# A triangular inverse, the RG-LRU's products and the rotations on VectorE alone, with a list schedule made in rounds

## The chip, the cores and the metric

The kernel runs on one core of one Trainium2 chip. The metric is the device time of one execution in microseconds. Each run of a kernel gives one time; a profiled execution also gives a trace and a page. Engine names in the rows: PE is TensorE (PEld its weight loads), DVE VectorE, ACT ScalarE, POOL GpSimd, SP SyncE.

## The reference

Two layers of a token mixer are computed for 128 context tokens and 512 latent tokens together (640 tokens, five tiles of 128). A layer does, in float32:

```python
mod = silu(c) @ w_mod + b_mod                 # shift, scale, gate
h = rms_norm(x) * (1 + scale) + shift
p = h @ w_in                                  # 640 x 3456
ya = rwkv7(p)         # two directions, a state of 64x64 for each of 4 heads
yb = window_attention(rope(p))                # and a sink
yc = rg_lru(conv(p))                          # two directions
yd = differential_attention(rope(p))
y = concat(ya, yb, yc, yd, each times its SiLU gate) @ w_out
x = x + gate * rms_norm(y)
```

The RWKV-7 recurrence s <- s*diag(w) - (s kk)(kk a)^T + v k^T is not run token by token: in chunks of 64 tokens it becomes matmuls and the inverse of a unit triangular 64x64 matrix for each chunk, head and direction.

## The kernel before

**Work.** Weights come as chunks of 512 KB through two `raw` buffers (`raw`, `weight`, L528 to L538), are split into a high and a low float32r half (`split`, L519: ScalarE or GpSimd rounds, L522 or L524, and VectorE subtracts, L525) and multiplied three times (hi*hi, hi*lo, lo*hi; `gemm_tm`, `gemm_fm`, all recorded by `mm`, L352). These dense matmuls are most of TensorE's work. `tm_chunk` makes six chunks of 256 columns token by token; chunks 2 and 4 (keys and queries of the differential attention) are copied from PSUM by ScalarE (L662) and rotated by `rope` (L579, five instructions at L586, L590, L591) on GpSimd for the four latent tiles; chunks 0 and 1 are rotated on VectorE straight from PSUM.

**Modulation.** `mod_chunk` and `mod_columns` (L412 to L432) multiply the two conditioning vectors with `w_mod`: eight matmuls a chunk with 32 columns of the array (`raw,cs` or `ZA,cs`), a copy, then two narrow products (`const,s`), from which VectorE writes `gadd` and `gmul` (L441, L443, L444). In layer 0 those for layer 1 are made between the dense matmuls.

**The inverse** (`rwkv_inv`, L1251). For each direction the attention matrices (FA,F matmuls of `rwkv_mats`, L1194, masked on VectorE at L1210) leave SBUF for DRAM (L1262) and come back with one 32x32 diagonal block a partition (L1264, 80 blocks). There a substitution runs over 31 columns: a product (L1278) and a subtraction (L1280) of outer products. `CUT = 24` splits each step's columns: a part goes to GpSimd, the rest (up to eight) to VectorE. The result is transposed (L1281), stored (L1282, L1283), reloaded (L1286, L1288) and joined to 64x64 by 32x32 matmuls (L1303, L1312). `rwkv_keys`, `rwkv_solve`, `rwkv_chain` and `rwkv_read` follow.

**RG-LRU** (`lru`, L1002). `LRU_CONV`, `LRU_Q`, `LRU_U`, `LRU_S` and `LRU_H` say for each half or direction whether GpSimd (1) or VectorE (0) does the convolution's taps, sqrt's argument, the gated input, its product and the sum of directions. On GpSimd a three-operand step is two instructions (`stt`, L990).

**Order.** `body` builds the program twice. The first build is only read: `plan` (L1873) collects each instruction's engine, a length by formula (`_length`), and its dependencies, and `_list_schedule` (L1800) lays them on the five in-order queues. An instruction's rank is the length of the longest chain from it to the end; at each moment the engine that is free takes the ready instruction of the highest rank. On TensorE it prefers to stay with matmuls that use 64 rows or fewer, or with those that use more (`half`; a change costs `TURN` = 0.1). It knows the shared time of VectorE and GpSimd (`port`). `follow` then ties each engine's instructions of the second build to that order. SP's queue issues all DMAs.

Of the kernel before, what the change touches and what calls it, by code (L numbers as in the profile page):

```python
# [101 lines left out]
DP1 = 1000  # L102
E_BANKS = (3, 6), (2,), (7,), (0, 1)
D_BANKS = (2, 3, 6, 7), (4,)
CUT = 24
F_WO = (9, 12)
LRU_BANKS = (4, 5)
D_ORDER = (4, 0, 1, 2, 3)
# [1 line left out]
F_TILES = (6, 7, 0, 1)  # L110
F_AT = (0, 2, 5, 8)
F_RO = (1, 3, 4, 5, 6)
LRU_CONV = (0, 1)
LRU_Q = (1, 1, 1, 1)
LRU_U = (0, 1, 0, 1)
LRU_S = (0, 1, 0, 1)
LRU_H = (1, 1)
W_F = 0
OUT_BANKS = (0, 2)
W_O = (0, 1, 0, 1)  # L120
# [139 lines left out]
class Net:  # L260
# [362 lines left out]
    def tm_evac(self, l, ch, i, ps):  # L623
        A, nc, O = self.A, self.nc, self.O
        tk = slice(i * 128, i * 128 + 128)
        if ch == 0:
            A.activation(self.bv[:, i, :], ps[:, 128:256], AF.Copy)
            r = self.t1([128, 128])
            if i == 4:
                A.activation(r, ps[:, 0:128], AF.Copy)  # L630
                nc.sync.dma_start(O["nwk"][l], r)
                nc.sync.dma_start(O["nwv"][l], self.bv[:, 4, :])
            else:
                self.rope(self.V, r, ps[:, 0:128], i, 2, 64, C_C64, C_S64)

            def rest():
                pt = self.pt([128, 128])
                self.P.transpose(pt, r, self.ident)
                A.activation(self.kT[:, i * 128:i * 128 + 128], pt, AF.Copy)
            return rest  # L640
        elif ch == 1:
            r = self.t1([128, 256])
            if i == 4:
                A.activation(r, ps, AF.Copy)
            else:
                self.rope(self.V, r, ps, i, 4, 64, C_C64, C_S64)

            def rest():
                pt = self.pt([128, 2, 128])
                for g in range(2):  # L650
                    self.P.transpose(pt[:, g, :], r[:, 128 * g:128 * g + 128], self.ident)
                A.activation(self.qT[:, :, tk], pt, AF.Copy)
            return rest
        elif ch in (2, 4):
            dst = self.at(self.turn("st", M_ST), [128, 256])
            if i == 4:
                A.activation(dst, ps, AF.Copy)
                if ch == 2:
                    nc.sync.dma_start(O["ndk"][l], dst)
            else:  # L660
                x = self.t1([128, 256])
                A.activation(x, ps, AF.Copy)  # L662
                self.rope(self.G, dst, x, i, 8, 32, C_C32, C_S32)
            nc.sync.dma_start(self.qkv[1 if ch == 2 else 0, :, i, :], dst)
        elif ch == 3:
            dst = self.at(self.turn("st", M_ST), [128, 256])
            A.activation(dst, ps, AF.Copy)
            nc.sync.dma_start(self.qkv[2, :, i, :], dst)
            if i == 4:
                nc.sync.dma_start(O["ndv"][l], dst)  # L670
        else:
            for p in range(2):
                rw = slice(64 * p, 64 * p + 64)
                A.activation(self.SV[rw, i, p], ps[rw, :].rearrange("p (h e) -> p h e", h=4), AF.Copy)
# [1049 lines left out]
SAME = 0.04  # L1724
# [36 lines left out]
    return 0.145 + 0.00104 * n  # L1761


def _shares(i):

    if _engine(i) == "Pool":
# [2 lines left out]
            and type(i).__name__[4:] not in ("Memset", "Reciprocal", "TensorReduce"))  # L1769


TURN = 0.1
STAY = 2.0


# [21 lines left out]
            self.k, self.busy = self.k + 1, 0.0  # L1797


def _list_schedule(names, engine, length, deps, size, half, port):  # L1800

    succ, left = {n: [] for n in names}, {}
    for n in names:
        left[n] = len(deps[n])
        for x in deps[n]:
            succ[x].append(n)
    seen = lambda n, s: (0.0 if engine[n] == "PE" else SAME) if engine[n] == engine[s] != "SP" else SEEN.get(engine[n], 0.0)
    todo, tail, free = [n for n in names if not left[n]], {}, dict(left)
    for n in todo:
        for s in succ[n]:  # L1810
            free[s] -= 1
            if not free[s]:
                todo.append(s)
    for n in reversed(todo):
        own = length[n] + (2.0 + size[n] / 320 if engine[n] == "SP" else 0.0)
        tail[n] = own + max((tail[s] + seen(n, s) for s in succ[n]), default=0.0)
    rank = {n: (-tail[n], k) for k, n in enumerate(names)}
    queues, turned, held = ENGINES + (None,), False, {"DVE": 0.0, "Pool": 0.0}
    clock = _Clock()
    idle, link, ready = dict.fromkeys(queues, 0.0), 0.0, dict.fromkeys(names, 0.0)  # L1820
    come, here, out = {e: [] for e in queues}, {e: [] for e in queues}, []
    for n in names:
# [2 lines left out]
    while len(out) < len(names):  # L1825
# [6 lines left out]
        if e == "PE":  # L1832
            if half[n] != turned:
# [5 lines left out]
                    heapq.heappush(here[e], (rank[n], n))  # L1839
                    n = x[1]  # L1840
                else:
                    t += TURN
            turned = half[n]
        if n in port:
            until = held["Pool" if e == "DVE" else "DVE"]
# [16 lines left out]
        if e == "SP":  # L1862
            link = max(link, t + 1.2) + size[n] / 320
            end = link + 0.6
        for s in succ[n]:
            ready[s] = max(ready[s], end + seen(n, s))
            left[s] -= 1
            if not left[s]:
                heapq.heappush(come[engine[s]], (ready[s], rank[s], s))
    return out  # L1870


def plan(I, O):  # L1873
# [13 lines left out]
    trace = {i.name: i for i in trace}  # L1887
    engine = {n: _engine(trace[n]) for n in names}
    length = {n: 0.08 if engine[n] == "SP" else _length(trace[n]) for n in names}
    half = {n: engine[n] == "PE" and list(trace[n].ins[0].ap)[0][1] <= 64 for n in names}  # L1890
    port = {n for n in names if _shares(trace[n])}
    size = {n: math.prod(k for _, k in trace[n].outs[0].ap) / 256 if engine[n] == "SP" else 0.0 for n in names}
    deps = {n: {d for d, _ in nc.dependency_edges(n)} & known for n in names}
# [52 lines left out]
```

## Time and profile before

| | |
|---|---|
| runs shown | 1174.52, 1188.54, 1189.49 us; median 1188.54 |
| the profiled execution | 1178.09 us, span 1176.3 us |
| granted TensorE clock, mean | 0.934 |
| busy: PE, PEld, DVE, ACT, POOL | 1056.7, 899.5, 701.6, 515.0, 381.7 us |
| chain that ended last, by engine | PE 62%, DVE 11%, ACT 8%, issue 8%, DMA 7%, POOL 3% |
| HBM read, written | 82.90 MB, 15.47 MB |

The span runs from the first to the last instruction. TensorE's ends are modelled and overlap, so a busy TensorE may still have slack; the granted clock tells which part of the time it ran at 2.4 and which at 1.2 GHz. A wait is put down to the releaser that came last.

### The profile page before, as it was taken

The page shows a single profiled execution, that of the slowest core. Times are in us where ns is not written, and L with a number is a line of the kernel's source. Part 1 is how long each engine was busy: PE and PEld are TensorE (multiplying, and loading weights), DVE is VectorE, ACT ScalarE, POOL GpSimd, SP SyncE. Part 2 cuts the span into 40 slices and gives each one's busy share as a digit, 9 for nine tenths or more (in the row PEclk, how much of TensorE's full clock was granted, in tenths as well). Part 3 has the DMA queues.
Part 4 walks back from the last instruction along what each step waited for, and adds up shares of the span by engine and source line. Part 5 has one row for each costly group of instructions (what it writes and reads, how often), then busy time and mean ns, then how long its engine had stood idle before and what let it go on. Part 6 is the DMA issues. An engine that isn't in the chain of part 4 may idle for free.

```text
span 1176.3 us, 24765 instructions
## 1 busy us (share of the span) xinstructions
PE 1056.7 (90%) x10166; PEld 899.5 (76%) x10166; DVE 701.6 (60%) x1646; ACT 515.0 (44%) x1154; POOL 381.7 (32%) x465
## 2 busy tenths in 40 slices
PE   4999988869988998899997999889997998999996
PEld 2798766758876786677996987688886787777796
DVE  4823477526567569478566248672667656967622
ACT  5426433124243547556226473223424354766410
POOL 0032443505780010015123366450577002112312
PEclk9999989769987999889998999987999899999898
DMA  9421344540323031014312102433031303101311
GB/s 367 163 70 69 120 128 118 178 118 9 86 76 81 7 104 43 19 36 139 109 72 90 55 30 83 113 108 95 13 92 65 81 7 120 45 19 37 126 55 54
DMA packets 60225, 99.97 MB, mean 85 GB/s; under 512 B 30736, under 2 KB 38672, under 8 KB 60112
## 3 DMA queue, kind: packets, MB, share of 16 engines
q1 hardware_dynamic: 60112, 98.39, 26.1%
q8 instruction: 80, 1.31, 0.5%
q14 instruction: 33, 0.27, 0.1%
HBM read 82.90 MB, written 15.47 MB: 84 GB/s over the span
## 4 chain that ended last, share of the span: by engine, by line
PE 62%; DVE 11%; ACT 8%; issue 8%; DMA 7%; POOL 3%; SPq 1%; POOLq 0%; ACTq 0%; DVEq 0%
PE banks L352 55%; PE banks L892 2%; PE banks L848 2%; DMA raw<-in_w_tm 1%; PE banks L783 1%; DMA F<-inv 1%; DMA inv<-F 1%; ACT FA L881 1%; DVE F L1280 1%; DMA raw<-in_w_m 1%; PE banks L1235 1%; POOL F L1562 1%; SPq L1286 1%; DMA inv<-ZA 1%; DVE WP L525 1%
## 5 line engine op out<-in xcount | busy, mean ns | idle before, releaser
L352 PE MATMUL banks<-HA,WP 128*128 128x384 f32 (+1 forms) x768 | 208.5, 339 | 7.7 <-DVE mt L701 5.4
L352 PE MATMUL banks<-WP,HA 128*128 128x256 f32 x880 | 186.8, 300 | 14.2 <-ACT WP L522 10.6
L352 PEld LDWEIGHTS banks<-WP,HA 128*128 128x128 f32 x880 | 145.1, 200 | 27.7 <-ACT WP L522 11.1
L352 PEld LDWEIGHTS banks<-HA,WP 128*128 128x128 f32 x768 | 140.0, 202 | 17.8 <-DVE mt L701 6.3
L352 PE MATMUL banks<-HB,WP 128*128 128x384 f32 (+1 forms) x384 | 126.5, 335 | 1.5 <-DVE rq L367 1.1
L352 PE MATMUL banks<-WP,HB 128*128 128x256 f32 x440 | 119.2, 298 | 0.0
L525 DVE TENSOR_TENSOR WP<-raw,WP 128x1024 fp32r<-128x1024 f32 x44 | 56.4, 1282 | 62.6 <-ACT WP L522 60.5
L352 PEld LDWEIGHTS banks<-WP,HB 128*128 128x128 f32 x440 | 82.8, 200 | 4.1 <-issue 3.3
L352 PEld LDWEIGHTS banks<-HB,WP 128*128 128x128 f32 x384 | 76.5, 201 | 5.2 <-issue 2.1
L352 PE MATMUL banks<-WQ,HA 128*128 128x256 f32 x320 | 77.3, 302 | 2.0 <-DVE WQ L525 0.9
L522 ACT ACTIVATE WP<-raw 128x1024 fp32r<-128x1024 f32 x46 | 48.4, 1059 | 64.4 <-PE banks L352 42.0
L352 PE MATMUL banks<-FA,F 64*128 64x128 f32 (+3 forms) x768 | 66.7, 277 | 5.0 <-DVE FA L1177 2.2
L352 PE MATMUL banks<-F,ZA 64*64 64x64 f32 (+2 forms) x1440 | 62.4, 228 | 5.9 <-DMA F<-inv 5.1
L352 PEld LDWEIGHTS banks<-F,ZA 64*64 64x64 f32 (+2 forms) x1440 | 55.1, 140 | 14.8 <-issue 6.8
L703 POOL TENSOR_TENSOR F<-F,mt 128x256 f32<-128x256 f32 (+1 forms) x16 | 19.2, 1199 | 137.3 <-DVE mt L701 119.8
L352 PEld LDWEIGHTS banks<-WQ,HA 128*128 128x128 f32 x320 | 58.0, 202 | 6.1 <-issue 3.1
L878 DVE TENSOR_REDUCE dm<-banks 128x2 f32<-128x1280 f32 (+1 forms) x40 | 50.9, 1273 | 19.0 <-PE banks L352 18.8
L352 PEld LDWEIGHTS banks<-FA,F 64*128 64x128 f32 (+2 forms) x768 | 47.9, 158 | 17.1 <-issue 7.5
L881 ACT ACTIVATE FA<-banks,dm 128x640 f32<-128x640 f32 (+1 forms) x80 | 56.4, 709 | 8.1 <-DVE dm L878 6.1
L352 PE MATMUL banks<-F 128*64 128x128 f32 (+3 forms) x256 | 44.0, 358 | 5.2 <-ACT F L763 3.8
L352 PE MATMUL banks<-WQ,HB 128*128 128x256 f32 x160 | 47.4, 301 | 0.0
L352 PE MATMUL banks<-HA,WQ 128*128 128x384 f32 (+1 forms) x192 | 45.6, 310 | 0.5 <-ACT K L733 0.5
(340 smaller groups left out, 2637.4 us busy)
## 6 DMA issues: line engine op xcount, KB each, us to landing
raw<-in_w_m SPq DMA_DIRECT2D x32, 512.0 KB, 3.5
raw<-in_w_fm SPq DMA_DIRECT2D x30, 512.0 KB, 3.4
raw<-in_w_tm SPq DMA_DIRECT2D x24, 512.0 KB, 3.7
raw<-in_w_o SPq DMA_DIRECT2D x16, 512.0 KB, 3.4
F<-in_x SPq DMA_DIRECT2D x10, 512.0 KB, 4.3
qkv<-F SPq DMA_DIRECT2D x30, 128.0 KB, 1.8
F<-qkv SPq DMA_DIRECT2D x6, 640.0 KB, 5.7
ZA<-in_w_m SPq DMA_DIRECT2D x6, 512.0 KB, 9.9
```

The lines of the kernel that those rows point to most:

```text
L352: self.P.matmul(out, lhsT, rhs, start=start, stop=stop)
L522: self.A.activation(hi, x, AF.Copy)
L525: (E or self.V).tensor_tensor(lo, x, hi.bitcast(F32), op=ALU.subtract)
L703: self.G.tensor_tensor(x, x, g, op=ALU.mult)
L783: P.transpose(pt[:, b * 128:(b + 1) * 128], eh[:, b * 128:(b + 1) * 128], self.ident)
L848: P.transpose(reg[0:96, j * 128:j * 128 + 128], tmp[:, i, m].rearrange("p a d -> p (a d)").bitcast(F32), self.ident)
L878: V.tensor_reduce(nm, sc, axis=AX.X, op=ALU.min)
L881: A.activation(e[:, m, :], sc[:, m, :], AF.Exp, bias=nm[:, m:m + 1], scale=-1.0, accum_out=s1 if m else s0)
L892: P.transpose(ps[:, k:k + 128], e[:, 0, k0 + k:k0 + k + 128], self.ident)
L1235: P.transpose(kt[:, p, m, :], self.KR[d, m][:, 2 * i + p, 0, :], self.ident)
L1280: E.tensor_tensor(N[:, rows, cs], N[:, rows, cs], t, op=ALU.subtract)
L1286: nc.sync.dma_start(blk(p, b, rw), nd[us].rearrange("u s t -> s u t"))
```

## The change

Three sets of constants move work from GpSimd to VectorE: `CUT` from 24 to 0, so that every step of the substitution stands whole on VectorE (for the forward direction `cut` is then 0, for the backward one 32); the five `LRU_` tables to 0; and the rotation of chunks 2 and 4. The number of VectorE's steps in an inverse stays 62, and their columns grow from 6312 to 10912.

The schedule is changed in two ways. TensorE's instructions now have four kinds (`_kind`: full, 64 rows or fewer, 32 columns or fewer, 64 columns or fewer), and a turn costs 0.3 where the 32-column kind is on one side, else 0.1. And `_list_schedule` does six rounds: `_forward` is the former pass; `_backward` lays the instructions on the queues from the end, in the reverse of the order in which the last forward pass ended them, and its (negative) times are the ranks of the next forward pass. The round with the earliest end by the schedule's own lengths is kept.

```diff
-CUT = 24
+CUT = 0
...
-LRU_CONV = (0, 1)
-LRU_Q = (1, 1, 1, 1)
-LRU_U = (0, 1, 0, 1)
-LRU_S = (0, 1, 0, 1)
-LRU_H = (1, 1)
+LRU_CONV = (0, 0)
+LRU_Q = (0, 0, 0, 0)
+LRU_U = (0, 0, 0, 0)
+LRU_S = (0, 0, 0, 0)
+LRU_H = (0, 0)
...
-                self.rope(self.G, dst, x, i, 8, 32, C_C32, C_S32)
+                self.rope(self.V, dst, x, i, 8, 32, C_C32, C_S32)
...
+def _kind(i):
+
+    m, k = _width(_operands(i)[1]), list(i.ins[0].ap)[0][1]
+    return 1 if k <= 64 else 2 if m <= 32 else 3 if m <= 64 else 0
...
-TURN = 0.1
+TURN = 0.1, 0.3
...
+ROUNDS = 6
...
+    rank, best = {n: -tail[n] for n in names}, None
+    for _ in range(ROUNDS):
+        out, ends = _forward(names, engine, length, deps, succ, size, half, port, {n: (rank[n], k) for k, n in enumerate(names)})
+        if best is None or max(ends.values()) < best[0]:
+            best = max(ends.values()), out
+        rank = _backward(names, engine, length, own, deps, succ, size, ends)
+    return best[1]
...
+def _backward(names, engine, length, own, deps, succ, size, ends):
+
+    left, ready, late = {n: len(succ[n]) for n in names}, dict.fromkeys(names, 0.0), {}
+    queues = ENGINES + (None,)
+    idle, link = dict.fromkeys(queues, 0.0), 0.0
+    come, here = {e: [] for e in queues}, {e: [] for e in queues}
+    for n in names:
+        if not left[n]:
+            heapq.heappush(come[engine[n]], (0.0, -ends[n], n))
+    while len(late) < len(names):
...
+        _, n = heapq.heappop(here[e])
+        end = t + own[n]
+        if e == "SP":
+            link = max(link, t) + size[n] / 320
+            end = link + 2.0
+        if e:
+            idle[e] = t + length[n] + NEXT.get(e, 0.0)
+        late[n] = -end
+        for x in deps[n]:
+            ready[x] = max(ready[x], end + _seen(engine, x, n))
+            left[x] -= 1
+            if not left[x]:
+                heapq.heappush(come[engine[x]], (ready[x], -ends[x], x))
+    return late
...
-                    t += TURN
+                    t += TURN[2 in (half[n], turned)]
...
-    half = {n: engine[n] == "PE" and list(trace[n].ins[0].ap)[0][1] <= 64 for n in names}
+    half = {n: engine[n] == "PE" and _kind(trace[n]) for n in names}
```

The order of all five engines is new. Three places are shown; in `rq`, `gadd`, `smm` and the like a number tells one buffer from the next.

VectorE in the first inverse (layer 0, forward), before: the fifth of five groups of the modulation (L441, L443, L444) stands between late steps of the substitution, which have eight columns.

```order
L1280 TENSOR_TENSOR F_77<-F_77 80x9x8
L441 TENSOR_SCALAR gadd_97<-banks,par_94 128x2
L1278 TENSOR_TENSOR F_77<-F_77 80x64
L443 TENSOR_SCALAR smm_2170<-banks,par_94 128x2
L1280 TENSOR_TENSOR F_77<-F_77 80x8x8
L444 TENSOR_SCALAR gmul_96<-smm_2170,par_94 128x2
```

The same engine and inverse after: the first of three groups, between steps that are as wide as they come.

```order
L1278 TENSOR_TENSOR F_77<-F_77 80x192
L591 TENSOR_TENSOR F_77<-F_77 128x4x16
L441 TENSOR_SCALAR gadd_97<-banks,par_94 128x2
L1280 TENSOR_TENSOR F_77<-F_77 80x24x8
L443 TENSOR_SCALAR smm_1835<-banks,par_94 128x2
L1278 TENSOR_TENSOR F_77<-F_77 80x207
L444 TENSOR_SCALAR gmul_96<-smm_1835,par_94 128x2
```

The groups are fewer inside the substitution, and the steps carry all columns.

TensorE where the first inverse's result is first used (32x32), before: the modulation's chunk (`raw`) and its narrow product stand ahead, dense matmuls (WP with HA, HB) around the first set of 40.

```order
L352 MATMUL banks<-WP_85,HB_84 128x256
L352 MATMUL banks<-raw_2205,cs_68 32x256 x4
L352 MATMUL banks<-const_66,s_118_2211 128x2 x2
L352 MATMUL banks<-WP_85,HA_83 128x256
L352 MATMUL banks<-F_77,ZA_79 32x32 x40
L352 MATMUL banks<-WP_85,HA_83 128x256
L352 MATMUL banks<-WP_85,HB_84 128x256
```

The same place after: one half of a modulation chunk (`raw_2052`) stands ahead of the first set, the other half (`raw_2058`) between the first and the second.

```order
L352 MATMUL banks<-WP_85,HB_84 128x256
L352 MATMUL banks<-raw_2052,cs_68 32x256 x4
L352 MATMUL banks<-F_77,ZA_79 32x32 x40
L352 MATMUL banks<-raw_2058,cs_68 32x256 x4
L352 MATMUL banks<-ZA_79,F_77 32x32 x40
L352 MATMUL banks<-const_66,s_110_2064 128x2
L352 MATMUL banks<-F_77,ZA_79 64x64 x32
```

Both sets stay whole, and no dense matmul is left between them. On SP's queue the load of `raw_2058` now stands behind the inverse's reload (L1286, L1288).

VectorE in the last inverse (layer 1, backward), before: the window attention's small steps (L755 to L775) and a gate (L710) stand between the steps.

```order
L1278 TENSOR_TENSOR WQ_7582<-WQ_7582,F_77 80x192
L755 TENSOR_REDUCE smw_9025<-banks 128x2
L1280 TENSOR_TENSOR F_77<-F_77,WQ_7582 80x24x8
L757 TENSOR_TENSOR smw_9027<-smw_9025,sink_335_9008 128x2
L1278 TENSOR_TENSOR WQ_7582<-WQ_7582,F_77 80x184
L758 TENSOR_SCALAR smw_9027<-smw_9027 128x2
L1280 TENSOR_TENSOR F_77<-F_77,WQ_7582 80x23x8
L775 TENSOR_TENSOR smw_9020<-smw_9020,smw_9017 128x2
L1278 TENSOR_TENSOR WQ_7582<-WQ_7582,F_77 80x176
L710 SCALAR_TENSOR_TENSOR F_77<-F_77,banks 128x384
```

The same inverse after: rotations of the differential attention's chunks (L586 to L591).

```order
L1280 TENSOR_TENSOR F_77<-F_77,WQ_7426 80x13x19
L591 TENSOR_TENSOR F_77<-F_77 128x16x8
L1278 TENSOR_TENSOR WQ_7426<-WQ_7426,F_77 80x240
L591 TENSOR_TENSOR F_77<-F_77 128x16x8
L1280 TENSOR_TENSOR F_77<-F_77,WQ_7426 80x12x20
L591 TENSOR_TENSOR F_77<-F_77 128x16x8
L1278 TENSOR_TENSOR WQ_7426<-WQ_7426,F_77 80x231
L1280 TENSOR_TENSOR F_77<-F_77,WQ_7426 80x11x21
L586 TENSOR_TENSOR F_77<-F_77,const_66 128x256
```

The window attention has mostly left this substitution, and the rotations that were GpSimd's have come in; L586 needs a copy of ScalarE (L662), which needs the chunk's matmuls on TensorE.

## Rows read from the trace of the kernel before

**Rows 1.** The page: busy time of each engine, and TensorE's granted clock in 40 slices.

```profile
PE 1056.7 (90%) x10166; PEld 899.5 (76%) x10166; DVE 701.6 (60%) x1646; ACT 515.0 (44%) x1154; POOL 381.7 (32%) x465
...
PEclk9999989769987999889998999987999899999898
```

**Rows 2.** Busy time by stretch: stretch, length, PE, PEld, DVE, ACT, POOL, granted clock, DMA share, GB/s.

```profile
199.00:265.00 66.00, 51.22 (x631) 42.12 (x631) 32.30 (x96) 17.10 (x36) 24.05 (x53) 0.74 0.49 145
318.00:383.00 65.00, 55.48 (x489) 46.04 (x488) 46.87 (x132) 25.79 (x71) 30.36 (x64) 0.84 0.26 71
755.00:816.00 61.00, 53.85 (x565) 48.81 (x563) 34.82 (x108) 18.21 (x41) 25.77 (x52) 0.84 0.38 114
873.00:937.00 64.00, 56.34 (x517) 47.11 (x517) 46.41 (x132) 27.07 (x73) 29.79 (x66) 0.89 0.25 72
```

**Rows 3.** Timeline, VectorE: first and last instruction of each substitution (start, length, what).

```profile
198.66 0.20 DVE L1278 TENSOR_TENSOR F<-F 80x31 f32<-80x31 f32 x1 [4.36 <-DMA F<-inv]
...
236.59 0.16 DVE L1280 TENSOR_TENSOR F<-F 80x8 f32<-80x8 f32 x1
...
317.73 0.92 DVE L1278 TENSOR_TENSOR WQ<-WQ,F 80x31 f32<-80x31 f32 x1 [9.09 <-DMA WQ<-inv]
...
366.50 0.16 DVE L1280 TENSOR_TENSOR F<-F,WQ 80x8 f32<-80x8 f32 x1
...
755.03 0.20 DVE L1278 TENSOR_TENSOR F<-F 80x31 f32<-80x31 f32 x1 [5.32 <-DMA F<-inv]
...
793.47 0.16 DVE L1280 TENSOR_TENSOR F<-F 80x8 f32<-80x8 f32 x1
...
873.19 0.91 DVE L1278 TENSOR_TENSOR WQ<-WQ,F 80x31 f32<-80x31 f32 x1 [7.15 <-DMA WQ<-inv]
...
920.30 0.16 DVE L1280 TENSOR_TENSOR F<-F,WQ 80x8 f32<-80x8 f32 x1
```

**Rows 4.** Timeline, VectorE, inside the first substitution.

```profile
218.43 0.22 DVE L441 TENSOR_SCALAR gadd<-banks,par 128x2 f32<-128x2 f32 x1 [2.96 <-PE banks L352]
...
225.23 0.22 DVE L441 TENSOR_SCALAR gadd<-banks,par 128x2 f32<-128x2 f32 x1 [3.91 <-PE banks L352]
...
226.30 0.26 DVE L1278 TENSOR_TENSOR F<-F 80x104 f32<-80x104 f32 x1
226.60 0.26 DVE L1280 TENSOR_TENSOR F<-F 80x104 f32<-80x104 f32 x1
...
233.02 0.22 DVE L441 TENSOR_SCALAR gadd<-banks,par 128x2 f32<-128x2 f32 x1 [3.95 <-PE banks L352]
```

**Rows 5.** Timeline, GpSimd: end of its part of the first; a rotation in the second.

```profile
223.82 0.23 POOL L1280 TENSOR_TENSOR F<-F,KPP 80x23 f32<-80x23 f32 x1
...
317.87 0.74 POOL L586 TENSOR_TENSOR F<-F,const 128x256 f32<-128x256 f32 x1
```

**Rows 6.** Timeline, TensorE, behind the first substitution.

```profile
246.19 0.58 PE L352 MATMUL banks<-WP,HA 128*128 128x256 f32 x1 [7.83 <-ACT WP L522]
...
247.85 0.39 PE L352 MATMUL banks<-F,ZA 32*32 32x32 f32 x4 [1.08 <-DMA F<-inv]
```

**Rows 7.** Timeline, TensorE, a visit of the modulation's matmuls among full ones.

```profile
213.97 0.28 PE L352 MATMUL banks<-WP,HB 128*128 128x256 f32 x1
214.09 0.40 PE L352 MATMUL banks<-WP,HA 128*128 128x256 f32 x2
214.42 1.07 PE L352 MATMUL banks<-raw,cs 128*32 128x256 f32 x16
215.42 0.39 PE L352 MATMUL banks<-WP,HB 128*128 128x256 f32 x1
215.65 0.40 PE L352 MATMUL banks<-WP,HA 128*128 128x256 f32 x2
```

**Rows 8.** Groups by line and form, VectorE: count, busy us, mean ns, idle before.

```profile
L590 DVE TENSOR_TENSOR F<-banks,const 128x128 f32<-128x128 f32 x16 | 4.2, 280 | 0.4 <-PE banks L651 0.4
...
L993 DVE SCALAR_TENSOR_TENSOR F<-F,par 128x643 f32<-128x643 f32 x6 | 5.3, 888 | 3.0 <-POOL F L1013 2.9
```

More of the change, by code (lines that the diff above doesn't have):

```diff
@@ L1797, in run, with _seen @@
             self.k, self.busy = self.k + 1, 0.0
+ROUNDS = 6
+def _seen(engine, n, s):
+    return (0.0 if engine[n] == "PE" else SAME) if engine[n] == engine[s] != "SP" else SEEN.get(engine[n], 0.0)
 def _list_schedule(names, engine, length, deps, size, half, port):
-    succ, left = {n: [] for n in names}, {}
+    succ = {n: [] for n in names}
     for n in names:
-        left[n] = len(deps[n])
         for x in deps[n]:
             succ[x].append(n)
-    seen = lambda n, s: (0.0 if engine[n] == "PE" else SAME) if engine[n] == engine[s] != "SP" else SEEN.get(engine[n], 0.0)
@@ L1808, in _list_schedule @@
-    todo, tail, free = [n for n in names if not left[n]], {}, dict(left)
+    left = {n: len(deps[n]) for n in names}
+    todo, tail = [n for n in names if not left[n]], {}
     for n in todo:
         for s in succ[n]:
-            free[s] -= 1
-            if not free[s]:
+            left[s] -= 1
+            if not left[s]:
                 todo.append(s)
+    own = {n: length[n] + (2.0 + size[n] / 320 if engine[n] == "SP" else 0.0) for n in names}
     for n in reversed(todo):
-        own = length[n] + (2.0 + size[n] / 320 if engine[n] == "SP" else 0.0)
-        tail[n] = own + max((tail[s] + seen(n, s) for s in succ[n]), default=0.0)
@@ L1817, in _list_schedule @@
-    rank = {n: (-tail[n], k) for k, n in enumerate(names)}
-    queues, turned, held = ENGINES + (None,), False, {"DVE": 0.0, "Pool": 0.0}
-    clock = _Clock()
+        tail[n] = own[n] + max((tail[s] + _seen(engine, n, s) for s in succ[n]), default=0.0)
+    rank, best = {n: -tail[n] for n in names}, None
[4 more added lines that the diff above has]
+        rank = _backward(names, engine, length, own, deps, succ, size, ends)
@@ new lines, in _list_schedule @@
+    return best[1]
[8 more added lines that the diff above has]
+    while len(late) < len(names):
+        t, k = min((idle[e] if here[e] else max(idle[e], come[e][0][0]), k) for k, e in enumerate(queues) if here[e] or come[e])
+        e = queues[k]
+        while come[e] and come[e][0][0] <= t:
+            _, r, n = heapq.heappop(come[e])
+            heapq.heappush(here[e], (r, n))
+        _, n = heapq.heappop(here[e])
[12 more added lines that the diff above has]
+    return late
@@ L1820, in _list_schedule, with _forward @@
+def _forward(names, engine, length, deps, succ, size, half, port, rank):
+    left = {n: len(deps[n]) for n in names}
+    queues, turned, held = ENGINES + (None,), 0, {"DVE": 0.0, "Pool": 0.0}
+    clock, ends = _Clock(), {}
     idle, link, ready = dict.fromkeys(queues, 0.0), 0.0, dict.fromkeys(names, 0.0)
@@ L1864, in _list_schedule @@
             end = link + 0.6
+        ends[n] = end
         for s in succ[n]:
-            ready[s] = max(ready[s], end + seen(n, s))
+            ready[s] = max(ready[s], end + _seen(engine, n, s))
             left[s] -= 1
@@ L1869, in _list_schedule @@
                 heapq.heappush(come[engine[s]], (ready[s], rank[s], s))
-    return out
+    return out, ends
 def plan(I, O):
```

## The prediction

> **What bounds the kernel now.** I read the page first: TensorE is busy for 1056.7 us of 1176.3, VectorE for 701.6, GpSimd for 381.7 [rows 1]. So TensorE bounds the kernel, and there is time on VectorE for more work. The granted clock is printed as 9 (90% or more) in most slices and as 6 to 8 in a few [rows 1]; in these, part of the time ran at 1.2 instead of 2.4 GHz. They lie mostly where the order runs through one of the four inverses (two layers, two directions). I therefore asked for the busy time of four stretches, each from the start of a substitution until its result is used: 66 + 65 + 61 + 64 = 256 us, TensorE busy 51.22 + 55.48 + 53.85 + 56.34 = 216.9, so idle for 39 us; the granted clock is 0.74, 0.84, 0.84 and 0.89 [rows 2]. At a clock of c, busy time B does the work of about B x c, so a further 13 + 9 + 9 + 6 = 37 us went to the lower level. Idle and clock together: 76 us in 256. The other 920 us lose much less for their length, so what the change does to these four stretches weighs most.
>
> **The substitution.** VectorE's first and last instruction of each stand at 198.66 and 236.59, 317.73 and 366.50, 755.03 and 793.47, 873.19 and 920.30 [rows 3]. With the last one's length that is 38.1, 48.9, 38.6 and 47.3 us, 172.9 in sum. GpSimd's part of the first ended at 224.05 [rows 5], 12.7 us ahead of VectorE's: VectorE ended last, though its share is the lighter in time. The reason is what stands between: it waited 2.96, 3.91 and 3.95 us in front of instructions of L441, which need a result of TensorE and have nothing to do with the inverse [rows 4]. Behind the first one TensorE stood still for 7.83 us (a weight chunk whose load is queued behind the inverse's store) and 1.08 us (the inverse itself) [rows 6].
>
> Price of a step alone: 104 columns take 0.26 us and the next instruction starts 0.30 after [rows 4], 8 columns take 0.16 [rows 3]. That is 0.15 + 0.04 between dependent ones + 1.04 ns a column. Before, VectorE's 62 instructions have 2 x 3156 columns in all (eight a step, or what there is): 62 x 0.19 + 6312 x 1.04 ns = 18.3 us. After, they are still 62 but with 2 x 5456 columns: 23.1 us. Between them, counted in the order, other instructions of VectorE stand: 22, 49, 38 and 49 before, 27, 49, 28 and 63 after. At 0.25 us each (L590 takes 0.28 with its overlap [rows 8]) that is 158 x 0.25 = 40 us before and 167 x 0.25 = 42 after. So VectorE's bare work is 4 x 18.3 + 40 = 113 before, and 172.9 - 113 = 60 us were waiting or instructions that were slowed. After it is 4 x 23.1 + 42 = 134, plus between 0 and 60: 134 to 194, which is 39 less to 21 more. I take half of the 60 (164, 9 us less), for two reasons. One part of the 60 is GpSimd's neighbourhood: the same 80x31 product took 0.20 us in the first substitution and 0.92 in the second [rows 3], where a rotation of 0.74 us ran on GpSimd [rows 5]; rotations and the inverse's own products leave GpSimd. The other part, waits like those of L441, stays possible: 3 instead of 5 of these stand inside the first substitution, but rotations have come into all four, and each of them needs a copy that follows a chunk of TensorE.
>
> The Trainium skill, Perfetto Trace Analysis, Optimizing Scalar/DVE Operations, says that GpSimd and VectorE share a read port, held as a lock, so that moving work between the two might not help. The 0.20 against 0.92 us agree. By that rule alone all slowed instructions would be cured and only the waits left, which would put the sum nearer its low end.
>
> What TensorE has to do meanwhile: between the last of the 40 attention-matrix matmuls (FA,F) and the first 32x32 stand 292, 325, 364 and 331 matmuls before, and 271, 355, 320 and 342 after (1312 and 1288). Most are dense ones of 0.12 us [rows 7]. The cover is nearly the same; I charge 4 us for what left it and must find a place elsewhere. The four stretches: -9 + 4 = -5 us, bounds -35 to +30. What is late next there is the second pair of matmuls of the first inverse: in the new order a modulation chunk, whose load now stands on SP's queue behind the inverse's reload, stands between the two; that may wait a microsecond, and lies inside the bounds.
>
> **Turns of the array.** The modulation's matmuls use 32 columns of the array, the transposed and 64-row ones half of it. A visit to the narrow kind [rows 7]: two dense ones from 214.09 should be done at 214.33, the narrow ones start at 214.42, 0.09 late; after them the first dense one takes 0.23 until the next starts, 0.11 more than 0.12. So one turn costs 0.10 us. Counted on TensorE's two orders with the four kinds of the new table, 575 turns become 483. 92 x 0.10 = 9.2 us less; 0 if they lay where TensorE waited anyway, 14 if a share falls in half-speed stretches. I take -9: outside the stretches TensorE is rarely idle, and nothing hides them.
>
> The Trainium skill, TensorEngine Tiling (Array Packing), Key Properties, says that a change of tiling mode drains the engine. The two delays agree with it; that page of the Trainium skill gives no time, so it changes no number here.
>
> **RG-LRU and rotations on VectorE.** Thirty LRU instructions come over, 26 of about 640 columns at up to 0.89 [rows 8] and four short ones at 0.5: 25 us. Sixteen rotations of five: 64 x 0.28 [rows 8] + 16 x 0.41 (128 columns more at 1.04 ns) = 24.5. The inverse adds 4 x 4.8 = 19. VectorE goes from 702 to some 770 us less what GpSimd cost it, two thirds of the span, and does not become the bound. The work lies beside dense matmuls; it is on no path that I can show to end last. I take 0, with -6 (GpSimd's slower instructions leave the LRU's chain) to +8 (VectorE late for a weight chunk's low half, L525).
>
> **The clock.** If the stretches have fewer holes, part of the 37 us at the lower level comes back. I take a sixth, -6, bounds -12 to +6.
>
> **Sum.** -5 - 9 + 0 - 6 = -20. The profiled execution took 1178.09 us (span 1176.3 and 1.8 around it): 1158. The runs of before lie between 1174.52 and 1189.49 with their median at 1188.54, so the profiled one is a quick one; against the median my forecast is 2.6% less, against its own execution 1.7%. A difference of about 2% is what a measurement of this kernel can tell from none. Bounds added: -67 and +44; eight in ten I put within 1130 to 1189.
>
> **Rivals.**
> 1. Bigger gain: both parts of the 60 us go. Then the substitutions end 39 us earlier, 4 to cover, the turns 9, the clock 6: 1178 - 50 = 1128. For it: VectorE's bare work is only 134 us, and it ended last before by waiting. Against: rotations have the same kind of wait.
> 2. No change: the waits inside stay, the turns lie beside other waits. Substitutions +5, cover +4, turns -9, clock -6: 1172. For it: 1.08 us is all that TensorE directly waits for the inverse in [rows 6], so a shorter chain may only uncover the next wait.
> 3. Slower: VectorE's queue blocks itself. Every rotation inside a substitution waits for the copy of a chunk that TensorE has not finished; since VectorE works in order, the inverse, now all on it, waits too, and TensorE runs dry at the end. Price: substitutions +21, cover +4 and 2 us of idle at each of four ends, clock +6, turns -9: +30, 1208. It decides from a sum of the four substitutions above 185 us. Against it: before, the same pattern with other instructions cost 60, already counted.
> 4. The change of order does not do what it says: the turns fall in the order, but TensorE's gaps do not: 1178 - 11 = 1167, inside the forecast's own range.
>
> **Chances.** Forecast with rival 4: 0.48 (1146 to 1170). Bigger gain 0.18, no change 0.22, slower 0.12. Faster by over 2% against the median of before (under 1164.8): all of the bigger gain and two thirds of the forecast, 0.50. Slower by over 2% (over 1212): half of rival 3 and the tail, 0.07. The rest, 0.43, within.
>
> **What would show it.** Right: the four substitutions sum to 155 to 170 us; the granted clock in their stretches is above 0.85 on the mean; TensorE's idle there is under 39; VectorE's busy time is 720 to 770 and GpSimd's below 200; an 80x31 product takes 0.2 us everywhere. Wrong: substitutions above 173 with waits in front of L586, or a span that fell while these stretches did not, which would put the gain into the rest of the order.

## The result, and the profile after

The changed kernel takes 1141.11 us (median of 1147.48, 1137.48, 1136.58 and 1144.74), the kernel before 1189.01 beside it: ratio 0.9626, 95% interval 0.9533 to 0.972. In a second comparison the two stood at 1136.13 and 1181.19: 0.9599, 0.9534 to 0.9664. The kernel is 3.7 to 4.0% faster; the forecast of 1158 us (2.6%) lies above, its range holds the result. The ratios leave out runs that are over 1.5% above the fastest of their kernel, at a lower granted clock; the medians in us, here and below, keep them.

The first view is the page, busy time by engine and TensorE's granted clock in 40 slices [rows 1].

```profile
PE 1041.1 (91%) x10166; PEld 901.7 (79%) x10166; DVE 733.2 (64%) x1756; ACT 515.1 (45%) x1154; POOL 203.9 (18%) x153
...
PEclk9799888988999999998998998989699999999898
```

The span is 1145.7 us. I split each span into three parts: idle (span less TensorE's busy time), work (busy time times the mean granted clock) and what the lower clock costs (the rest of the busy time). Before: 119.6 + 987.0 + 69.7 (clock 0.934). After: 104.6 + 973.4 + 67.7 (0.935). Idle gave 15 us, work 14, the clock 2. This profile is of the slowest of the four executions; a profile of the same kernel from the second comparison has 103.6 + 972.7 + 57.7, span 1134.0. Idle and work repeat to 1 us, the clock's part to 10 only, so I compare kernels by the first two, by the ratios, and by the granted clock of all their runs. Its mean is 0.943 and 0.948 for the changed kernel in the two comparisons, and 0.927 for the kernel before in the second. So 2 us is too little for the clock: of the 45 us of the second comparison idle gave 16 and work 14 by the profiles, which leaves some 15 (an estimate) for the clock.

The second view is VectorE's timeline, first and last instruction of the four substitutions, which answers to [rows 3].

```profile
186.16 0.20 DVE L1278 TENSOR_TENSOR F<-F 80x31 f32<-80x31 f32 x1 [2.96 <-DMA F<-inv]
...
215.80 0.19 DVE L1280 TENSOR_TENSOR F<-F 80x31 f32<-80x31 f32 x1
...
296.63 0.21 DVE L1278 TENSOR_TENSOR WQ<-WQ,F 80x31 f32<-80x31 f32 x1 [2.48 <-DMA WQ<-inv]
...
330.20 0.19 DVE L1280 TENSOR_TENSOR F<-F,WQ 80x31 f32<-80x31 f32 x1
...
728.90 0.20 DVE L1278 TENSOR_TENSOR F<-F 80x31 f32<-80x31 f32 x1 [3.85 <-DMA F<-inv]
...
760.83 0.19 DVE L1280 TENSOR_TENSOR F<-F 80x31 f32<-80x31 f32 x1
...
837.47 0.20 DVE L1278 TENSOR_TENSOR WQ<-WQ,F 80x31 f32<-80x31 f32 x1 [7.09 <-DMA WQ<-inv]
...
871.23 0.19 DVE L1280 TENSOR_TENSOR F<-F,WQ 80x31 f32<-80x31 f32 x1
```

They last 29.8, 33.8, 32.1 and 34.0 us, 129.7 in sum, where it was 172.9. The 80x31 product takes 0.2 us at every place. What went is mostly waiting. VectorE's waits between the first and the last instruction of each, as its timeline prints them, sum to 40.7 us before and to 6.1 after. The lengths of the 4 x 62 steps sum to 85.0 and 84.7, though they carry more columns now, and other instructions between them to 64.9 and 58.5 (these lengths overlap a little). A rotation that came over waits for its copy once:

```profile
316.59 0.42 DVE L586 TENSOR_TENSOR F<-F,const 128x256 f32<-128x256 f32 x1 [0.61 <-ACT F L662]
```

The third view is busy time by stretch, from each substitution's start to the first 32x32 matmul that uses its result. Columns: stretch, length, PE, PEld, DVE, ACT, POOL, granted clock, DMA share, GB/s. The kernel before, and the changed one:

```profile
198.70:247.85 49.15, 34.98 (x279) 27.62 (x278) 28.13 (x89) 9.96 (x21) 22.00 (x50) 0.79 0.57 166
317.70:374.43 56.73, 47.20 (x300) 38.81 (x298) 42.95 (x123) 23.63 (x68) 30.66 (x65) 0.85 0.26 69
755.00:802.44 47.44, 40.35 (x332) 36.73 (x330) 31.23 (x102) 14.23 (x33) 24.67 (x50) 0.93 0.44 129
873.20:928.23 55.03, 47.37 (x321) 39.05 (x319) 42.04 (x123) 24.50 (x68) 29.55 (x65) 0.91 0.26 71
sum 208.35, PE 169.91 PEld 142.21 DVE 144.35 ACT 72.32 POOL 106.88; mean PE 42.48 PEld 35.55 DVE 36.09 ACT 18.08 POOL 26.72
```

```profile
186.16:226.78 40.62, 30.63 (x254) 24.05 (x252) 27.65 (x93) 11.40 (x27) 3.42 (x4) 0.89 0.53 152
296.63:339.63 43.00, 41.62 (x321) 37.37 (x319) 38.69 (x133) 16.14 (x44) 0.76 (x2) 1.00 0.41 115
728.90:770.07 41.17, 33.44 (x276) 30.73 (x275) 29.97 (x96) 11.88 (x28) 2.38 (x4) 0.92 0.44 133
837.47:881.10 43.63, 42.68 (x323) 38.00 (x321) 38.76 (x141) 19.06 (x54) 1.39 (x2) 0.96 0.38 108
sum 168.42, PE 148.38 PEld 130.15 DVE 135.06 ACT 58.48 POOL 7.95; mean PE 37.10 PEld 32.54 DVE 33.77 ACT 14.62 POOL 1.99
```

The stretches are 40 us shorter. But 21.5 us of that is TensorE's busy time, which is now spent elsewhere. Idle fell from 38.4 (208.35 - 169.91) to 20.0 us, so 18.4 against 15 in the whole span: all the idle that went, went here. What the lower clock costs there (busy time times one less the clock, stretch by stretch) fell from 21.5 to 7.8 us. Idle and clock together are 60.0 us before and 27.8 after, and 27.8 in the second profile too: 32 us less, most of the gain.

The fourth view is TensorE's timeline behind the first substitution [rows 6].

```profile
224.75 1.08 PE L352 MATMUL banks<-raw,cs 128*32 128x256 f32 x8 [2.23 <-DMA raw<-in_w_m]
226.78 0.42 PE L352 MATMUL banks<-F,ZA 32*32 32x32 f32 x4 [0.95 <-DMA F<-inv]
228.27 2.34 PE L352 MATMUL banks<-F,ZA 32*32 32x32 f32 x76 [1.06 <-DMA F<-inv]
230.79 1.08 PE L352 MATMUL banks<-raw,cs 128*32 128x256 f32 x8 [0.18 <-DMA raw<-in_w_m]
```

In place of 7.83 and 1.08 us there are 2.23, 0.95 and 1.06. What is late next is the modulation's chunk, as forecast, but ahead of the first 32x32 set; its second half waits 0.18.

### The profile page after: what moved, and what is told of

Its sections match the earlier page's. It is cut to its first block, busy times and chain, and to the rows that moved or that the text cites. A ratio compares the mean times of both kernels' runs of the same rounds, so it can differ in the third digit from the quotient of the medians.

```text
span 1145.7 us, 24542 instructions
## 1 busy us (share of the span) xinstructions
PE 1041.1 (91%) x10166; PEld 901.7 (79%) x10166; DVE 733.2 (64%) x1756; ACT 515.1 (45%) x1154; POOL 203.9 (18%) x153
## 4 chain that ended last, share of the span: by engine, by line
PE 56%; DVE 19%; ACT 8%; issue 7%; DMA 7%; SPq 1%; POOL 1%; POOLq 0%; ACTq 0%; DVEq 0%
PE banks L352 50%; DVE WP L525 2%; DVE F L1280 2%; DVE dm L878 1%; PE banks L783 1%; PE banks L892 1%; PE banks L848 1%; DMA F<-qkv 1%; DVE F L1278 1%; DMA inv<-ZA 1%; DVE FA L886 1%; DMA raw<-in_w_o 1%; DVE ZA L1210 1%; DMA F<-inv 1%; ACT WP L522 1%
## 5 line engine op out<-in xcount | busy, mean ns | idle before, releaser
L352 PE MATMUL banks<-HA,WP 128*128 128x384 f32 (+1 forms) x768 | 200.9, 331 | 5.8 <-DVE mt L701 4.7
L352 PEld LDWEIGHTS banks<-HA,WP 128*128 128x128 f32 x768 | 134.2, 194 | 15.3 <-DVE mt L701 5.9
L352 PE MATMUL banks<-HB,WP 128*128 128x384 f32 (+1 forms) x384 | 121.1, 324 | 1.5 <-DVE rq L367 1.1
L352 PE MATMUL banks<-WP,HB 128*128 128x256 f32 x440 | 121.9, 292 | 0.0
L352 PE MATMUL banks<-FA,F 64*128 64x128 f32 (+3 forms) x768 | 77.4, 311 | 12.7 <-DVE FA L1180 5.2
L352 PEld LDWEIGHTS banks<-FA,F 64*128 64x128 f32 (+2 forms) x768 | 60.4, 189 | 24.9 <-issue 16.1
L352 PEld LDWEIGHTS banks<-HB,WP 128*128 128x128 f32 x384 | 73.6, 194 | 3.7 <-DVE HB L525 1.9
L525 DVE TENSOR_TENSOR WP<-raw,WP 128x1024 fp32r<-128x1024 f32 x44 | 56.3, 1282 | 24.7 <-ACT WP L522 23.5
L352 PEld LDWEIGHTS banks<-F,ZA 64*64 64x64 f32 (+2 forms) x1440 | 55.3, 139 | 13.5 <-DMA F<-inv 5.2
L352 PE MATMUL banks<-HA,WQ 128*128 128x384 f32 (+1 forms) x192 | 49.3, 323 | 2.6 <-ACT K L733 2.6
L1354 POOL TENSOR_TENSOR FA<-const,eC 128x256 f32<-128x256 f32 (+1 forms) x24 | 15.5, 666 | 176.1 <-PE banks L1235 176.1
L352 PE MATMUL banks<-K,HA 128*128 128x256 f32 x160 | 42.8, 300 | 0.4 <-ACT K L522 0.4
```

Source lines behind the costliest of these rows:

```text
L352: self.P.matmul(out, lhsT, rhs, start=start, stop=stop)
L525: (E or self.V).tensor_tensor(lo, x, hi.bitcast(F32), op=ALU.subtract)
L1354: G.tensor_tensor(KR[:, :, :, 0, :], eye.unsqueeze(1).unsqueeze(1).to_broadcast([128, 2, n, 64]), self.eC[:, d, m, 2 * i0:2 * i0 + 2 * n]. ...
```

## The experiments

My first theory: the new places make the gain, by the shorter substitutions. Its rival: the new order does. The ratio is to the kernel before, run beside it on the same chip, and "clock" is the mean granted clock of the runs that the ratio counts; the other columns are of one profiled execution each. Three groups were run side by side, each on a chip of its own: place_only to rounds12, changed to same_order, long_chain to stay252. The kernel before had a clock of 0.934, 0.927 and 0.932 in the three. "In stretches" is idle between a substitution's start and the first 32x32 matmul; turns are counted in TensorE's order between the four kinds of matmul.

| kernel | ratio (95%) | substitutions, us | idle, us | in stretches | work, us | turns | clock |
|---|---|---|---|---|---|---|---|
| before | 1 | 172.9 | 119.6 | 38.4 | 987.0 | 575 | 0.927 to 0.934 |
| place_only | 0.9946 (0.9903 to 0.999) | 130.0 | 104.5 | 28.1 | 992.2 | 623 | 0.935 |
| sched_only | 0.9893 (0.9819 to 0.9967) | 163.9 | 110.1 | 27.3 | 970.9 | 521 | 0.929 |
| one_round | 0.9856 (0.9798 to 0.9915) | 130.0 | 117.8 | 24.1 | 964.1 | 477 | 0.930 |
| rounds12 | 0.974 (0.9666 to 0.9814) | 126.8 | 97.9 | 18.0 | 971.3 | 488 | 0.932 |
| changed, again | 0.9599 (0.9534 to 0.9664) | 127.6 | 103.6 | 21.2 | 972.7 | 483 | 0.948 |
| chain_only | 0.9749 (0.9668 to 0.9829) | 155.6 | 112.2 | 22.6 | 967.3 | 486 | 0.929 |
| stay4 | 0.9767 (0.9684 to 0.9849) | 128.8 | 117.2 | 27.5 | 966.4 | 464 | 0.932 |
| same_order | 0.9729 (0.9652 to 0.9807) | 134.7 | 114.2 | 27.6 | 975.0 | 483 | 0.941 |
| long_chain | 0.9952 (0.991 to 0.9995) | 160.0 | 123.4 | 39.9 | 973.1 | 483 | 0.930 |
| round5 | 0.9686 (0.9605 to 0.9767) | 130.3 | 107.8 | 21.0 | 965.5 | 480 | 0.932 |
| stay308 | 0.9518 (0.9446 to 0.959) | 122.1 | 100.3 | 22.6 | 970.7 | 483 | 0.952 |
| stay252 | 0.9529 (0.9456 to 0.9602) | 128.7 | 93.1 | 19.9 | 973.0 | 457 | 0.950 |

**The places alone, and the list schedule alone.** place_only is the kernel before with

```diff
-CUT = 24
+CUT = 0
...
-LRU_CONV = (0, 1)
+LRU_CONV = (0, 0)
...
-                self.rope(self.G, dst, x, i, 8, 32, C_C32, C_S32)
+                self.rope(self.V, dst, x, i, 8, 32, C_C32, C_S32)
```

(the other LRU tables to zeros as well); sched_only is the changed kernel with these edits reversed.

> The kernel before with the new places alone (inverse, RG-LRU and rotations on VectorE), and its old list schedule. Theory: the gain is VectorE's freedom from GpSimd, so the places alone bring most of it: 1140 to 1160 us, the four substitutions 125 to 150 us in sum, an 80x31 product 0.2 us everywhere. Rival (the gain is the new order: rounds and turn prices): 1172 to 1190 us, though the substitutions are short.

> The kernel before with the new list schedule alone (rounds, backward passes, four kinds with two turn prices), the work on the engines of before. Theory: 1175 to 1195 us, substitutions still 155 us or more in sum, since GpSimd and VectorE still slow one another. Rival (the order): 1140 to 1160 us.

Measured: 1168.55 and 1161.12 us, beside 1172.48 for the kernel before. Neither theory stands. The places shorten the substitutions as far as the whole change does (130.0 against 129.7) and bring 0.5%. The schedule leaves them at 163.9 and brings 1.1%. Together the two would make 1.6%; the change has 3.7 to 4.0. By these ratios more than half of the gain is in neither part alone (at the far ends of the intervals the two parts reach 2.8%, and the whole begins at 2.8).

The table says what is missing. Idle and work fall by 9.9 us with the places alone, by 25.6 with the schedule alone, and by 28.6 and 30.3 with both (two profiles), so of these nothing is missing. The clock is: 0.935 and 0.929 with one part, where the kernel before has 0.934 beside them, 0.943 and 0.948 with both. In the four stretches the places alone do much of what the change does: idle and clock cost 37.8 us there, and 45.7 with the schedule alone, where it was 60.0 and becomes 27.8. The waits inside the substitutions go with the places alone (4.4 us) and stay with the schedule alone (35.9). What the places gain in the stretches is lost again in part: work is 5 us more in the whole span, and the lower clock costs 10 us more outside the stretches (one profile of each). What in the order sets the clock outside the stretches no run shows.

**One round, twelve rounds, five rounds.**

```diff
-ROUNDS = 6
+ROUNDS = 1
```

and 12 and 5 in the same line. With one round the kinds and turn prices stay and the backward passes go. Of twelve, a round behind the sixth is taken: its order is another one (488 turns).

> The changed kernel with one round in place of six; kinds and turn prices stay. It takes the backward passes out. Theory: within 10 us of the changed kernel (1136 to 1150). Rival: the backward passes carry the gain, 1165 or more.

> The changed kernel with twelve rounds in place of six, so another of many similar orders is taken. Theory: it shows how much the time moves from one such order to the next with everything else equal, 1130 to 1150 us. Rival (rounds carry the gain): 1125 us or less.

> The changed kernel with five rounds in place of six: the order of the fifth pass, which the planner rates almost like the sixth. Theory (one order of this kind differs from the next by chance of what meets what): anywhere in 1132 to 1158 us. Rival (each backward pass improves the order and the planner's rating holds on the chip): within 4 us of the changed kernel.

Measured: 1157.21, 1145.11 and 1142.72 us. One round is outside the theory's interval and short of the rival's: against the changed kernel the passes are worth 0.9856 - 0.96 or some 2.5%, against rounds12, which ran beside it, 1.2%. The page of one_round against that of place_only, which differ by kinds and turn prices alone, shows what these do (place_only first):

```profile
PE 1060.0 (91%) x10166; PEld 900.3 (77%) x10166; DVE 729.1 (63%) x1756; ACT 513.5 (44%) x1154; POOL 206.0 (18%) x153
```

```profile
PE 1036.7 (90%) x10166; PEld 896.0 (78%) x10166; DVE 730.0 (63%) x1756; ACT 513.3 (44%) x1154; POOL 203.5 (18%) x153
```

The same 10166 matmuls take 23.3 us less of busy time (at clocks of 0.936 and 0.930, 28.1 of work) with 146 turns fewer, but idle grew by 117.8 - 104.5 = 13.3. That grouping by kind delays chains is the likely reason, not a shown one. The backward passes take that idle back (117.8 to 104) and lose 9 of work, which leaves 4 to 6 us of the 16 to 21 between one round and the changed kernel. The rest goes with the clock (0.930 against 0.943 and 0.948). In the four stretches idle falls by 3 to 4 us, and what the clock costs there from 16.9 to 7.8 and 6.6; the rest is spread, and I did not trace it to one place. Twelve and five rounds show the scatter between like orders: both lie above the changed kernel's medians, and their intervals reach into that of its first comparison (rounds12's just misses the second's). Their sums of idle and work (1069.2 and 1073.3 us) are below the changed kernel's 1076.3 and 1078.0; their clock is lower. Whether round five is really slower stays open: at 1.6 us above one median and 6.6 above the other it fits theory and rival.

**The inverse alone on VectorE.** chain_only is the changed kernel with RG-LRU and rotations on GpSimd again (the lines above, without CUT). **The same order, other engines.** same_order makes the plan with everything on VectorE and then executes the rotations and eight products (the expectation's four, in each of two layers) on GpSimd, each engine in the planned order (`PLAN` is true while the order is made):

```diff
-                self.rope(self.V, dst, x, i, 8, 32, C_C32, C_S32)
+                self.rope((self.G, self.V)[PLAN], dst, x, i, 8, 32, C_C32, C_S32)
...
-    order = plan(I, O)
+    global PLAN, LRU_S, LRU_H
+    order, PLAN = plan(I, O), False
+    LRU_S, LRU_H = (0, 1, 0, 1), (1, 1)
```

> The changed kernel once more, beside the runs that follow, so that all four stand against the same runs of the kernel before. Expected ratio to before 0.960 to 0.980 (1141 of 1189 us in the first comparison, where before's own runs lay high).

> The changed kernel with the RG-LRU's products and the rotations put back on GpSimd; the inverse alone stays on VectorE, the new list schedule stays. Theory (the inverse's single queue is what the new places give, the other two are nothing by themselves, as the prediction's 0 for them): within 8 us of the changed kernel, substitutions 130 to 145 us in sum. Rival (GpSimd's rotations slow VectorE's steps): substitutions above 150 us and 12 us or more slower than the changed kernel.

> The changed kernel's order kept on every engine, with the sixteen rotations and four of the RG-LRU's products executed by GpSimd instead of VectorE (the order is made with them on VectorE). TensorE's instructions come in exactly the same order. Theory (where these run matters little when the order stays): 0 to 8 us slower, substitutions 130 to 145 us. Rival (the two engines slow each other wherever they meet): 12 us or more slower, substitutions above 150 us.

Measured: 1136.13 for the changed kernel, 1152.14 and 1149.66 for the two. My theory fell both times: rotations and RG-LRU on GpSimd cost 16.0 us with a new order and 13.5 with the order held, though the substitutions of same_order (134.7 us) stay in the theory's interval. In chain_only they take 155.6, with 23.5 us of waits inside. The timelines tell a part of how. The second substitution of same_order, VectorE and then GpSimd at the same time:

```profile
295.59 0.27 DVE L1280 TENSOR_TENSOR F<-F,WQ 80x112 f32<-80x112 f32 x1
295.90 0.71 DVE L1278 TENSOR_TENSOR WQ<-WQ,F 80x135 f32<-80x135 f32 x1
296.64 0.44 DVE L1280 TENSOR_TENSOR F<-F,WQ 80x135 f32<-80x135 f32 x1
297.12 0.46 DVE L1278 TENSOR_TENSOR WQ<-WQ,F 80x156 f32<-80x156 f32 x1
```

```profile
295.66 0.80 POOL L586 TENSOR_TENSOR F<-F,const 128x256 f32<-128x256 f32 x1 [6.80 <-ACT F L662]
296.42 0.99 POOL L590 TENSOR_TENSOR F<-F,const 128x128 f32<-128x128 f32 x2
297.37 1.03 POOL L591 TENSOR_TENSOR F<-F 128x128 f32<-128x128 f32 x2
```

and the same place in the changed kernel, where the rotation is VectorE's:

```profile
298.79 0.30 DVE L1278 TENSOR_TENSOR WQ<-WQ,F 80x135 f32<-80x135 f32 x1
299.12 0.30 DVE L1280 TENSOR_TENSOR F<-F,WQ 80x135 f32<-80x135 f32 x1
299.45 0.32 DVE L1278 TENSOR_TENSOR WQ<-WQ,F 80x156 f32<-80x156 f32 x1
...
300.52 0.34 DVE L1280 TENSOR_TENSOR F<-F,WQ 80x175 f32<-80x175 f32 x1
300.90 0.36 DVE L1278 TENSOR_TENSOR WQ<-WQ,F 80x192 f32<-80x192 f32 x1
301.17 0.42 DVE L586 TENSOR_TENSOR F<-F,const 128x256 f32<-128x256 f32 x1
301.51 0.35 DVE L1280 TENSOR_TENSOR F<-F,WQ 80x192 f32<-80x192 f32 x1
301.78 0.28 DVE L590 TENSOR_TENSOR F<-F,const 128x128 f32<-128x128 f32 x1
301.98 0.36 DVE L1278 TENSOR_TENSOR WQ<-WQ,F 80x207 f32<-80x207 f32 x1
```

Until GpSimd starts, the steps are alike (0.27); from there the 80x135 product takes 0.71 and its subtraction 0.44 in place of 0.30. The Trainium skill, Perfetto Trace Analysis, Optimizing Scalar/DVE Operations, says that the two engines share a read port of SBUF, which one kind of VectorE operation holds as a lock. The slowing agrees with a shared port; the rows do not show one engine waiting out the whole of the other's instruction. All steps of the four substitutions sum to 98.5 us against 85.0 in the changed kernel's second profile. But the rotations have left VectorE, so the substitutions of same_order are only 7 us longer in sum (134.7 against 127.6), and TensorE's idle is 10.6 us higher, 6.4 of it in the stretches. So the slowed steps explain about half of the 13.5 us. The rest I did not separate; a rotation's five instructions take 0.80 + 0.99 + 1.03 us on GpSimd, and whoever waits for one may wait longer.

**Fewer turns.** stay4 doubles the bound within which an instruction of the present kind goes ahead:

```diff
-                    other = [x for x in here[e] if half[x[1]] == turned and x[0][0] < rank[n][0] + STAY]
+                    other = [x for x in here[e] if half[x[1]] == turned and x[0][0] < rank[n][0] + 2 * STAY]
```

> The changed kernel with TensorE's order held in one kind of matmul for longer (an instruction of the present kind goes ahead when its rank is up to 4 us later, not 2): 464 turns between the four kinds in place of 483. Theory (a turn costs 0.1 to 0.2 us of TensorE's busy time, but holding back a late chain costs too): busy time times clock 2 to 4 us lower, the time within 10 us of the changed kernel. Rival (turns alone make the gain): faster by 3 us or more.

Measured: 1153.19 us, 17 more than the changed kernel. Work is 6 us less, more than expected, and idle 13.6 more. Turns alone don't make the gain; it is outside the theory's interval too. Idle and work together make 7 of the 17 us, the clock is lower too (0.932 against 0.948), and it is one order: that holding back chains costs this is likely, not shown.

**A longer chain in the same order.** long_chain adds an instruction to each step of the inverse and leaves the order of everything else as it is (the added ones are made behind the plan and take no part in it):

```diff
...
+                    if not PLAN:
+                        E.tensor_scalar(t, t, 1.0, None, op0=ALU.mult)
                     E.tensor_tensor(N[:, rows, cs], N[:, rows, cs], t, op=ALU.subtract)
```

> The changed kernel's order kept on every engine, with one more instruction of VectorE in each step of the four inverses (the product times 1.0, in place, between the product and its subtraction): 124 more at some 0.29 us, so substitutions of 160 to 170 us in sum, as long as the prediction took them. Theory (in this order the dense work beside an inverse is only as long as the short substitution, so a longer one is waited for): 18 to 40 us slower than the changed kernel, the idle time at the four ends. Rival (TensorE has other work there, the substitution's length is hidden, as it was when the places alone were changed): under 8 us slower.

Measured: 1172.5 us, 31 to 36 more than the changed kernel's medians (by the ratios 3.3 to 3.5%, some 40 us), for 30.3 us more of substitution (160.0 - 129.7). Busy time by stretch:

```profile
186.70:232.77 46.07, 33.92 (x256) 27.78 (x254) 34.84 (x124) 11.37 (x27) 2.30 (x4) 0.81 0.46 134
303.50:355.77 52.27, 44.26 (x303) 39.78 (x301) 46.28 (x164) 16.02 (x44) 0.76 (x2) 0.87 0.32 91
744.30:791.99 47.69, 35.95 (x277) 32.92 (x276) 37.80 (x127) 11.99 (x28) 2.42 (x4) 0.86 0.39 115
859.40:910.76 51.36, 43.39 (x321) 37.70 (x320) 47.53 (x173) 19.71 (x54) 0.80 (x2) 0.97 0.32 92
sum 197.39, PE 157.51 PEld 138.18 DVE 166.45 ACT 59.09 POOL 6.28; mean PE 39.38 PEld 34.54 DVE 41.61 ACT 14.77 POOL 1.57
```

Idle there is 39.9 us against 20.0, and the clock is down to 0.81, 0.87, 0.86 and 0.97. What the lower level costs there is 18.5 us against 7.8. The two differences, 20 and 11, make 31 us, the loss by the medians. In this order the longer substitution is paid for about microsecond by microsecond: TensorE's dense work beside it is as long as the short substitution and no longer. The theory stands here, with the substitutions at the lower end of its 160 to 170 us.

**Orders that the planner rates better.** stay308 has ROUNDS = 13 and STAY = 3.08, stay252 has 11 and 2.52.

> The changed kernel with thirteen rounds and a bound of 3.08 us for staying in a kind of matmul or off a held port, the order that the planner rates best of some two hundred tried, far ahead of the changed kernel's. Theory (the rating is too rough at this distance): 1128 to 1150 us. Rival (the rating holds on the chip): 1125 us or less, better than both kernels.

> The same with eleven rounds and a bound of 2.52 us: 457 turns of the array in place of 483, rated second best. Theory: 1128 to 1150 us, busy time times clock 3 to 5 us below the changed kernel's. Rival: 1125 us or less.

Measured: 1122.3 and 1123.12 us, ratios 0.9518 and 0.9529. Both rivals win: the rating holds at this distance, and both are faster than the kernel before by 4.7 to 4.8%. All eight runs (1116.42 to 1127.9) lie below all eight of the changed kernel (from 1133.19), though not beside it; the ratios differ from its 0.9599 by 0.7 to 0.8%, with intervals that overlap. The two get there differently, so neither turns nor the stretches alone explain them: stay252 has the least idle (93.1) and the fewest turns, stay308 has the clock:

```profile
PE 1019.6 (91%) x10166; PEld 887.1 (79%) x10166; DVE 741.4 (66%) x1756; ACT 514.8 (46%) x1154; POOL 206.0 (18%) x153
...
PEclk9899999969997999999898998999999799999999
```

(mean 0.952, 48.9 us lost to the lower level against 57.7 and 67.7 in the changed kernel's two profiles). The rating is not fine: a later round is kept only if it is rated better, so it also puts rounds12 ahead of the changed kernel, and the chip's medians do not.

## Why the prediction was right, and where it was not

- **The bound.** TensorE bounds the kernel still, and the four stretches hold the idle that went. The claim that VectorE would end at 720 to 770 us of busy time and not be the bound was right (733.2). GpSimd was to be below 200 and is at 203.9.
- **The substitution, -9 us: mis-sized.** The step that failed is "I take half of the 60". The 60 were what I took them for: 40.7 us of waits, and steps that took 85.0 us where their price alone gives 63.5. But I kept the waits as possible, because rotations would bring the same kind, and the waits are what went (6.1 left, 0.61 of it in front of a rotation that came over). So all of it went: 129.7 us, 43 less, with 19 us more for the wider steps. It is even under the 134 that I called bare, because that figure had 0.25 us for each instruction between two steps. The timeline above shows 0.08 and 0.22 (last section).
- **Cover, +4, making -5 for the stretches: mis-sized.** Idle there fell by 18.4 and the clock's cost by 13.7, so 32 in place of these 5 and the clock's 6. Yet the shorter chain isn't enough: with the places alone, planned by the former list schedule, idle falls as much in the whole span (15.1 us), but turns rise to 623, work by 5 us, and the time falls by 0.5% only.
- **Turns, 92 x 0.10 = -9: too small, and likely right in kind.** Work fell by 13.6 us, which would be 0.15 for each of these 92; place_only against one_round gives 28.1 / 146 = 0.19. But sched_only loses 16.1 us of work with 54 turns fewer, and the changed kernel with 38 fewer still has 2 us more. Among orders of the new planner work (964 to 975 us) doesn't follow the count closely either, so that the turns are what the work went with is not shown. stay4 shows that such a saving can be lost twice over.
- **RG-LRU and rotations, 0 with -6 to +8: wrong in size.** same_order puts the rotations and eight of the products back at 13.5 us, twice the lower bound. I had named one cause, the neighbourhood of GpSimd, but charged it to the substitution alone; it explains about half.
- **The clock, -6: mis-sized.** 2 us in one profile, 12 in the other, some 15 by the runs of the second comparison. The granted clock of the stretches was to be above 0.85 and is 0.94 on the mean; in the shorter stretches used here the kernel before has 0.87, so that sign alone says little.
- **The backward passes had no term.** I counted what the order changed (turns, interleaved instructions, cover) and found no price for a better order as such. It is worth 1.2 to 2.5%, by the order it is measured with.

The sum was -20 us, the profiles show -31 and -42, the ratios 3.7 to 4.0% of some 1180, or 44 to 47. The terms for the substitution and the turns were too small, and so, by the runs, was the clock's. The range holds the time because it was wide; the 1146 to 1170 us that the chances gave the forecast do not. Of the rivals, the first (1128, both parts of the 60 go) had the mechanism inside the substitutions, and the time ended between it and the forecast. The second's time (1172) is near that of the places with the former list schedule (1168.55), but not by its argument, that a shorter chain only uncovers the next wait: idle fell there, and work rose. The third, VectorE blocking itself, was wrong: it decides above 185 us of substitutions, and a rotation's instruction between two steps costs 0.08 to 0.22 us. The fourth was wrong: TensorE's gaps did shrink.

## What to carry to other kernels

A shorter chain is worth what the order makes of it: 43 us less brought 0.5% under the former list schedule, which had planned for the shorter chain, and 30 us more cost all they last when they came into an order planned without them. So judge new places together with the planner, plan again after each change, and draw several orders: here orders from the new planner with the same places lay between 0.952 and 0.986. An experiment that compares one order with one other carries that scatter. To price a placement alone, hold every engine's order and move only the engine. And look at the granted clock of all runs: like orders differed here by the clock more than by idle and work.

## What was not expected of the hardware

- An independent VectorE instruction between two dependent ones cost 0.20 us less than its own length. In the changed kernel's rows above, from 300.52 to 300.90 a step with 175 columns takes 0.38 us; from 300.90 to 301.51 one with 192 columns and a 128x256 product between takes 0.61, from 301.51 to 301.98 one with a 128x128 product 0.47. A step with 192 columns alone is 0.39 (0.35 and a gap of 0.04), so they cost 0.22 and 0.08, where their own lengths are 0.42 and 0.28. A long one saves no more: a step with 240 columns and an L525 subtraction of 1.21 us behind it takes 1.45 (305.11 to 306.56, rows not shown), 1.01 more than the step alone (0.44).
- The same kernel in two executions differs by 11.7 us of span, of which 10.0 is the granted clock (0.935 and 0.944), while idle and work agree within 1 us.
